# A transformer block kernel on Trainium2: low rotated keys padded with zeros to 128 rows, norms' projections in pairs, gathered rows used three steps behind their issue, spilled tiles from unit 9 on

## The chip, the cores and the metric

The kernel runs on one core of one Trainium2 chip. The metric is the device time of one execution in microseconds. Before the change it is 2821.38 us, the median of three runs (2819.73 to 2827.19).

## What is computed

The program takes a sequence of 512 tokens of width 1024 through three blocks. All arithmetic is in fp32, and the kernel keeps it by splitting each operand of a product into a high and a low part and adding three products.

1. A block with chunked gated linear attention, then a SwiGLU feed-forward.
2. A block with latent attention (MLA), then a SwiGLU feed-forward. The scores of a head are cut here to what the change touches:

```python
proj = h @ w_in
cq, ckv, k_rope = jnp.split(proj, [384, 640], axis=-1)
q_rope = apply_rope(q_rope, cos, sin)
k_rope = apply_rope(k_rope[:, :, None, :], cos, sin)[:, :, 0, :]
s = (einsum('bqhd,bkhd->bhqk', qn_b, k_nope) + einsum('bqhd,bkd->bhqk', qr_b, k_rope)) * scale
p = softmax(where(mask, s, -inf)); o = p @ v
```

The head has 128 unrotated and 64 rotated columns; the rotated key is shared by all 8 heads.

3. A block with a pooling and a convolution branch, and then a mixture of 16384 experts of one neuron each. Each token scores two sets of 128 keys per head (8 heads), takes the best 16 sums, and computes

```python
u = jnp.take(expert_u, experts, axis=0)
act = jax.nn.gelu(einsum('chkd,cd->chk', u, hc))
v = jnp.take(expert_v, experts, axis=0)
out = einsum('chk,chkd->cd', gate * act, v)
```

Adaptive layer norms (gain, shift and gate from a conditioning vector) stand ahead of every mixer and feed-forward; a final norm ends it.

## The kernel before

The activations lie with the width on the partitions and the tokens on the free axis, as 8 tiles `x[k]` of 128x512. `split` (L234) makes of an fp32 tile a high part by a cast on ACT and a low part by a subtraction on DVE (or on the engine `eng`). `mm3` (L274 to L276) multiplies in three matmuls: high by high, high weight by low input, low weight by high input. Weights stream in units of 1 MB: SP issues the load of `raw` (L267, and L1115 for the experts), and `parts` (L238) splits it in two halves, `whi` on ACT and `wlo` on DVE, both L240. There are two `raw` buffers, four `whi` and four `wlo`.

**Order of the work.** Each engine has a queue of its own, and a scheduler decides in which order the instructions stand in it; `high_priority` moves an instruction forward in it, `issue_after` holds one back. An engine works off its queue in order, so that an instruction which waits holds up all behind it.

**Norms.** `rsqrt` (L347) finds the inverse root of each token's mean square in three rounds of small DVE instructions (L355 to L357), `ry` and `rt` being 128x2. `bcast` (L365) spreads it over the partitions by PE transposes (L369). Then `modulated` makes `tmp`, `hh` and `hl` for the 8 input tiles (L424 to L426). `ahead` (L281) is the projection that follows a norm: four output tiles of it are computed while the norm of the second half of the tokens is still under way. It takes one bank after the other, with all 8 input tiles for each. Its weights' low parts are made by POOL (`eng=G_`). `ahead` is used at five sites; at the last, `w_query_2`, the table `POOL_LO` names POOL as well.

**Latent attention.** `norm_mla` rotates the shared key (L843 to L846) and splits it into `krh` and `krl`, 128x512 each, with the 64 rows twice, one copy for even and one for odd heads. `queries` (L865) makes for each head a tile `qs` which holds the high part in 64 rows and the low part in the other 64. `weigh` (L889) sums the scores of each block of 128 queries in five matmuls (L900 to L904); the third of them (L902) takes only the 64 rows `rr` of `qs` and `krl`. Softmax follows on DVE and ACT (L905 to L912), then the product with the values in `attend` (L915 to L931).

**Experts.** For the first 368 tokens the experts are computed densely. `up` (L1118) multiplies a unit of `ust` (256 experts) with the tokens, applies Gelu and keeps two tiles `a`. There is room for 16 of these (`NA`), so 8 units are computed ahead, and 12 later ones, in `SPILL`, are computed early, written to memory and brought back by `back` (L1132). The main loop (L1433) goes through 16 groups of 8 tiles: it loads the gates of the group into `gt` by SP (L1441), multiplies them into the tiles (L1443), splits these into `wh_` and `wl_` (L1444), and for each half of the output multiplies with two units of `vex` (`unit`, L1112) into four banks, which DVE then adds to `x` (L1462). After each half, `ups` computes or brings back two units for a later group.

**Gathered tokens.** The other 144 tokens take their experts' rows one at a time in `gathered` (L1352): POOL gathers `rows` by an indirect DMA (L1378), DVE multiplies with the token (L1382) in the first 144 steps, or adds into `y` (L1392) in the second 144. There are five `rows` buffers. `pace` (L1416) issues the steps evenly between the units, after a start of `FIRST = 3`.

## Time and profile before

| | |
|---|---|
| median of 3 runs | 2821.38 us (2819.73 to 2827.19) |
| profiled execution | 2822.08 us |
| its span in the trace | 2820.3 us |
| TensorE's mean granted clock | 0.986 |
| PE busy | 2706.4 us, 96% of the span, 14889 matmuls |
| DVE busy | 2107.8 us, 75% |
| ACT busy | 1072.3 us, 38% |
| POOL busy | 759.5 us, 27% |
| DMA | 560.62 MB, 199 GB/s in the mean |

The profile is of one execution. Times are microseconds from the start of its span; a line such as L902 is a line of the kernel before. PE is the matmul queue of TensorE, PEld its weight loads. Matmuls are pipelined, so their durations overlap, and the distance from start to start tells how fast they pass. The granted clock is a share of the full clock: TensorE has two levels, 1.2 and 2.4 GHz, so 0.83 over a window means that the lower one held for a third of it. An idle time stands in brackets ahead of the instruction that ended it, with what released it. The latent attention's heads lie at 750 to 880 us; the experts' selection and first group at 1900 to 2000 us; the main loop of experts from there to 2790 us.

### The profile page before, as it was taken

To read this page: it belongs to the slowest core of one execution; us is meant where nothing else is said; L and a number is where in the kernel's file an instruction comes from. 1 tells how busy PE (TensorE), PEld (TensorE's weight loads), DVE (VectorE), ACT (ScalarE), POOL (GpSimd) and SP (SyncE) were. 2 spreads that over 40 slices of the span, in tenths; PEclk is the share of its full clock that TensorE was granted. 3 is DMA by queue.
4 is the path that set the end of the run, shared out by engine and by line. 5 is a ranking of instruction groups with operands and counts; after the bars stand their busy time and mean duration, and the time that the engine had idled before them with its cause. 6 is when DMAs were issued, how large, how long until landed. Compare 5 with 4: busy or idle time off the path is not lost. (4 is left out here: it accounts for less than half of the span.)

```text
span 2820.3 us, 38954 instructions
## 1 busy us (share of the span) xinstructions
PE 2706.4 (96%) x14889; PEld 2435.0 (86%) x14889; DVE 2107.8 (75%) x4011; ACT 1072.3 (38%) x1530; POOL 759.5 (27%) x652
## 2 busy tenths in 40 slices
PE   6799999999999999999999999998899999999998
PEld 4677888888778888888888889998899999999998
DVE  8874755556776654548956897788998898888996
ACT  4443322223443322234443246653333333333332
POOL 4631100001011000001521410004555444445550
PEclk9999999999999999999999999999999999999999
DMA  6441355553212555522223236666999999988993
GB/s 262 148 137 60 135 193 180 189 191 109 75 45 75 179 181 177 181 88 91 90 90 105 77 125 211 208 201 254 345 347 352 351 335 329 349 335 319 350 350 130
DMA packets 184363, 560.62 MB, mean 199 GB/s; under 512 B 13248, under 2 KB 66912, under 8 KB 157680
## 3 DMA queue, kind: packets, MB, share of 16 engines
q1 hardware_dynamic: 128528, 356.74, 35.9%
q0 software_dynamic: 55296, 201.35, 19.7%
q8 instruction: 117, 1.92, 0.3%
q14 instruction: 70, 0.57, 0.1%
q10 hardware_dynamic: 352, 0.03, 0.0%
HBM read 527.32 MB, written 30.75 MB: 198 GB/s over the span
## 5 line engine op out<-in xcount | busy, mean ns | idle before, releaser
L240 ACT CAST whi<-raw 128x1024 fp32r<-128x1024 f32 x510 | 535.8, 1052 | 1260.8 <-PE mm L275 782.0
L275 PE MATMUL mm<-hl,whi 128*128 128x512 f32 (+2 forms) x2544 | 898.5, 354 | 9.7 <-DVE hl L426 8.9
L274 PE MATMUL mm<-hh,whi 128*128 128x512 f32 (+2 forms) x2544 | 898.2, 354 | 4.1 <-ACT hh L425 3.5
L276 PE MATMUL mm<-hh,wlo 128*128 128x512 f32 (+2 forms) x2544 | 897.1, 354 | 0.1
L240 DVE TENSOR_TENSOR wlo<-raw,whi 128x1024 fp32r<-128x1024 f32 x472 | 580.7, 1231 | 288.4 <-ACT whi L240 277.8
L275 PEld LDWEIGHTS mm<-hl,whi 128*128 128x128 f32 x2544 | 481.1, 189 | 58.4 <-DVE hl L426 10.7
L274 PEld LDWEIGHTS mm<-hh,whi 128*128 128x128 f32 x2544 | 480.7, 189 | 51.4 <-ACT hh L425 4.3
L276 PEld LDWEIGHTS mm<-hh,wlo 128*128 128x128 f32 x2544 | 481.1, 189 | 46.9 <-issue 0.8
L1378 POOL DMA_INDIRECT rows<-vex,eidx x144 | 219.3, 1523 | 210.2 <-DVE y L1392 192.5
L1378 POOL DMA_INDIRECT rows<-uex,eidx x144 | 209.2, 1453 | 214.6 <-DVE rows L1382 164.5
L319 POOL DMA_DIRECT2D araw<-ada x96 | 51.1, 533 | 555.4 <-DVE araw L312 538.1
L1392 DVE SCALAR_TENSOR_TENSOR y<-rows,act,y 128x1024 f32<-128x1024 f32 x142 | 181.3, 1277 | 7.4 <-DMA rows<-vex,eidx 6.9
L1382 DVE SCALAR_TENSOR_TENSOR rows<-rows,hn 128x1024 f32<-128x1024 f32 x144 | 170.0, 1219 | 15.4 <-DMA rows<-uex,eidx 15.4
L240 POOL TENSOR_TENSOR wlo<-raw,whi 128x1024 fp32r<-128x1024 f32 x38 | 91.2, 2405 | 279.2 <-ACT whi L240 234.4
L312 DVE SCALAR_TENSOR_TENSOR araw<-araw,sc 128x1024 f32<-128x1024 f32 x128 | 157.1, 1251 | 5.6 <-DMA araw<-ada 5.5
L275 PE MATMUL mm<-fl,whi 128*128 128x512 f32 (+1 forms) x396 | 145.1, 366 | 0.0
L276 PE MATMUL mm<-fh,wlo 128*128 128x512 f32 (+1 forms) x396 | 144.7, 365 | 0.0
L274 PE MATMUL mm<-fh,whi 128*128 128x512 f32 (+1 forms) x396 | 144.7, 365 | 0.0
L740 DVE TENSOR_TENSOR s<-s,mm 128x512 f32<-128x512 f32 x42 | 28.9, 688 | 133.6 <-PE mm L276 133.0
L448 DVE SCALAR_TENSOR_TENSOR x<-mm,mod,x 128x512 f32<-128x512 f32 (+1 forms) x66 | 43.9, 667 | 85.8 <-PE mm L276 85.7
L1311 ACT ACTIVATE stage<-acc 128x512 f32<-128x512 f32 x92 | 91.4, 1104 | 37.3 <-PE acc L1308 26.7
L1308 PE MATMUL acc<-oa,ob 128*128 128x128 f16 x736 | 101.6, 296 | 0.2
(1382 smaller groups left out, 4709.6 us busy)
## 6 DMA issues: line engine op xcount, KB each, us to landing
raw<-wst SPq DMA_DIRECT2D x127, 1024.0 KB, 5.0
raw<-ust SPq DMA_DIRECT2D x64, 1024.0 KB, 6.3
raw<-vex SPq DMA_DIRECT2D x64, 1024.0 KB, 7.4
araw<-ada POOLq DMA_DIRECT2D x96, 512.0 KB, 4.6
gd<-stage SPq DMA_DIRECT2D x23, 1024.0 KB, 4.6
gt<-gd SPq DMA_DIRECT2D x16, 1472.0 KB, 9.2
araw<-ada SPq DMA_DIRECT2D x32, 512.0 KB, 4.3
aw<-ada SPq DMA_DIRECT2D x16, 512.0 KB, 8.5
```

The source lines that it names most:

```text
L240: state["split"] = (A_.copy(hi, src), (eng or V).tensor_sub(lo, src, hi.bitcast(F32)))
L274: T_.matmul(out_, wh, ah, start=first, stop=False)
L275: T_.matmul(out_, wh, al, start=False, stop=False)
L276: state["mm"] = T_.matmul(out_, wl, ah, start=False, stop=last)
L312: op(out=w, in0=w, scalar=1.0, in1=sc, op0=ALU.mult, op1=ALU.mult, accum_out=out_)
L319: (G_ if l else SP).dma_start(raw, w[n * P:(n + 1) * P, :])
L448: return V.scalar_tensor_tensor(x[n][:, cs], p[:, cs], gate[:, n:n + 1], x[n][:, cs], op0=ALU.mult, op1=ALU.add)
L1308: T_.matmul(p[:, t * P:(t + 1) * P], ob[:, q, :, t], oa[i][:, q, :, t], start=i == 0, stop=i == 1)
L1311: A_.mul(st[:, :, t1:t1 + 4].rearrange("p j t -> p t j"), p.rearrange("p (t j) -> p t j", t=4), 1.0 / GSC)
L1378: G_.indirect_dma_start(out=r, out_offset=None, in_=uex if up_ else vex, in_offset=bass.IndirectOffsetOnAxis(ap=eidx[:, n:n + 1] if n < P ...
L1382: V.scalar_tensor_tensor(r, r, 1.0, hn if n < P else hx, op0=ALU.mult, op1=ALU.mult, accum_out=act[:, n:n + 1])
L1392: V.scalar_tensor_tensor(z, r, act[:, n:n + 1], z, op0=ALU.mult, op1=ALU.add)
```

## The change

Five things change; line numbers of the kernel after are two or three higher at first, 8 at `queries`, 16 and more in `gathered`.

1. **Low rotated keys.** `krl` becomes two tiles, in one buffer `kz` that has the tag `araw`. The one for even heads has zeros in rows 64 to 127, the one for odd heads in rows 0 to 63. L902 then multiplies all 128 rows. The subtraction is done in two pieces of 64 rows, and POOL writes the zeros.
2. **Projections of the norms.** `ahead` no longer names POOL for the low parts, so DVE makes them at four of the five sites (`POOL_LO` still holds at `w_query_2`). The four banks are computed in two pairs, with the input tile in the outer loop.
3. **Gathered rows.** Each step issues the gather of its row and uses the row that was issued `LAG = 3` steps before; `FIRST` is 4.
4. **Gates.** `gt` is loaded by ACT's queue, for the group after the one that was just multiplied. The products and splits have the priority `GPRI = 300`.
5. **Units.** `SPILL` is spread over units 16 to 63 in place of 8 to 63. The values of the experts come from `vst`, an array laid out on the host so that each partition's 8 KB of a unit are contiguous; before, four runs of 2 KB were read from `vex`.

```diff
+LAG = 3
+GPRI = 300
-FIRST = 3
+FIRST = 4
-SPILL = [NA // 2 + (2 * i + 1) * (P // 2 - NA // 2) // (2 * NSP) for i in range(NSP)]
+SPILL = [NA + (2 * i + 1) * (P // 2 - NA) // (2 * NSP) for i in range(NSP)]
...
-        ws = [[blk(name, eng=G_) for _ in ah] for _ in range(4)]
+        ws = [[blk(name) for _ in ah] for _ in range(4)]
...
-            for p, w in zip(pre, ws):
-                for k, (wh, wl) in enumerate(w):
-                    mm3(p[:, cs], wh, wl, ah[k][:, cs], al[k][:, cs], k == 0, k == len(ah) - 1)
+            for two in range(0, 4, 2):
+                for k in range(len(ah)):
+                    for p, w in zip(pre[two:two + 2], ws[two:two + 2]):
+                        mm3(p[:, cs], *w[k], ah[k][:, cs], al[k][:, cs], k == 0, k == len(ah) - 1)
...
-        krh, krl = [mp.tile([P, S], F32R, name=f"kr{i}") for i in range(2)]
-        split(krh, krl, kr)
+        krh = mp.tile([P, S], F32R, name="krh")
+        A_.copy(krh, kr)
+        kz = mn.tile([P, D], F32R, tag="araw", bufs=ARAW, name="kz")
+        krl = kz[:, :S], kz[:, S:]
+        for i, t in enumerate(krl):
+            on, off = slice(i * 64, i * 64 + 64), slice(64 - i * 64, 128 - i * 64)
+            G_.memset(t[off].bitcast(F32), 0.0)
+            V.tensor_sub(t[on], kr[on], krh[on].bitcast(F32))
...
-                T_.matmul(sc[:, :n], qx[rr, qs], krl[rr, :n], start=False, stop=False)
+                T_.matmul(sc[:, :n], qx[:, qs], krl[h % 2][:, :n], start=False, stop=False)
...
-                for i in range(2 * (P + EX)):
-                    n = i % (P + EX)
-                    up_ = i < P + EX
-                    r = ep.tile([P, D], F32, tag="rows", bufs=NROW, name="rows")
-                    G_.indirect_dma_start(out=r, out_offset=None, in_=uex if up_ else vex,
...
+                rows = []
+                for i in range(2 * (P + EX) + LAG):
+                    if i < 2 * (P + EX):
+                        n = i % (P + EX)
+                        r = ep.tile([P, D], F32, tag="rows", bufs=NROW, name="rows")
+                        G_.indirect_dma_start(out=r, out_offset=None, in_=uex if i < P + EX else vex,
...
+                        rows.append(r)
+                    if i < LAG:
+                        yield
+                        continue
+                    r = rows.pop(0)
+                    n = (i - LAG) % (P + EX)
+                    up_ = i - LAG < P + EX
...
-            per = (2.0 * (P + EX) - FIRST) / (todo - LAST)
+            per = (2.0 * (P + EX) + LAG - FIRST) / (todo - LAST)
...
+            def gate_load(g):
+                gt = er.tile([P, 3072], F32, tag="gt", bufs=1, name="gt")[:, :TD * JG] \
+                    .rearrange("p (s j t) -> p s j t", j=JG, t=TS)
+                A_.dma_start(gt, gd[g])
+                return gt
+            gt = gate_load(0)
...
-                        SP.dma_start(gt, gd[j // JG])
-                    V.tensor_mul(a, a, gt[:, :, j % JG, :])
-                    split(wh, wl, acts[j])
+                    with tc.high_priority(GPRI):
+                        V.tensor_mul(a, a, gt[:, :, j % JG, :])
+                        split(wh, wl, acts[j])
...
+                if g + 1 < P // GJ:
+                    gt = gate_load(g + 1)
...
-                        v = unit(vex[r0:r0 + 4 * P, half * 512:(half + 1) * 512]
-                                      .rearrange("(j p) d -> p j d", p=P), rearr=True)
+                        v = unit(vst[g * GJ // 4 + j4, half])
...
+        "vst": a["expert_v_2"][0].reshape(P // 4, 4, P, 2, 512).transpose(0, 3, 2, 1, 4).reshape(P // 4, 2, P, 2048),
```

The scheduler's order moves with it at three places.

On DVE, at the first norm that `ahead` follows (`rt`, `ry` the small tiles of the inverse root, `sa` the sum of squares, `tmp` and `hl` the modulated input, `wlo` a weight's low part), there stood before:

```order
L355 TENSOR_TENSOR rt<-ry 128x2
L356 TENSOR_TENSOR rt<-rt,rv 128x2
L357 SCALAR_TENSOR_TENSOR ry<-rt,ry 128x2
L395 TENSOR_TENSOR sa<-sa,sq 128x256
L424 SCALAR_TENSOR_TENSOR tmp<-x_84,sca,acc 128x256
L424 SCALAR_TENSOR_TENSOR tmp<-x_85,sca,acc 128x256
L424 SCALAR_TENSOR_TENSOR tmp<-x_86,sca,acc 128x256
L426 SCALAR_TENSOR_TENSOR hl_100<-tmp,mod_108,hh_92 128x256
```

and now:

```order
L358 TENSOR_TENSOR rt<-ry 128x2
L359 TENSOR_TENSOR rt<-rt,rv 128x2
L242 TENSOR_TENSOR wlo<-raw,whi 128x1024
L360 SCALAR_TENSOR_TENSOR ry<-rt,ry 128x2
L398 TENSOR_TENSOR sa<-sa,sq 128x256
L427 SCALAR_TENSOR_TENSOR tmp<-x_84,sca,acc 128x256
L427 SCALAR_TENSOR_TENSOR tmp<-x_85,sca,acc 128x256
L427 SCALAR_TENSOR_TENSOR tmp<-x_86,sca,acc 128x256
L427 SCALAR_TENSOR_TENSOR tmp<-x_87,sca,acc 128x256
L242 TENSOR_TENSOR wlo<-raw,whi 128x1024
L429 SCALAR_TENSOR_TENSOR hl_100<-tmp,mod_108,hh_92 128x256
```

Two subtractions of weights have come into DVE's row, one ahead of the last `ry`, one ahead of the first `hl`; before, POOL had them.

On DVE, at the start of the experts' main loop (`a` the activated tiles, which L1443 multiplies with the gates, `wl__` their low parts, and between them the last steps of the selection), there stood before:

```order
L240 TENSOR_TENSOR wlo<-raw,whi 128x1024
L1188 TENSOR_TENSOR g<-top 128x128
L1201 TENSOR_SCALAR du<-po 128x128 x2
L240 TENSOR_TENSOR wl__16343<-a,wh__16342 128x368
L1443 TENSOR_TENSOR a<-a,gt 128x368 x3
L1191 TENSOR_REDUCE sx<-g 128x8
L1443 TENSOR_TENSOR a<-a,gt 128x368
```

and now:

```order
L242 TENSOR_TENSOR wlo<-raw,whi 128x1024
L1196 TENSOR_TENSOR g<-top 128x128
L1209 TENSOR_SCALAR du<-po 128x128 x2
L1464 TENSOR_TENSOR a<-a,gt 128x368 x3
L242 TENSOR_TENSOR wl__16336<-a,wh__16335 128x368
L1199 TENSOR_REDUCE sx<-g 128x8
L1209 TENSOR_SCALAR du<-po 128x128
```

`wl__16336` is the low part of the group's first tile, and all eight products now stand ahead of it; before, `wl__16343` was the third tile's, and the first two had been split between the products.

On PE, around the first group's two halves (`acc<-wh__`, `acc<-wl__` the group's products, `mm<-hh_`, `mm<-hl_` an `up` unit for a later group). Before, 24 matmuls of `up` stood between the halves, and 48 between the second half and group 1, whose first tile is `wh__16870`:

```order
L276 MATMUL acc<-wh__16367,wlo 128x368
L274 MATMUL mm<-hh_92,whi 128x368
...
L276 MATMUL mm<-hh_99,wlo 128x368
L274 MATMUL acc<-wh__16330,whi 128x368
L275 MATMUL acc<-wl__16331,whi 128x368
...
L276 MATMUL mm<-hh_99,wlo 128x368
L274 MATMUL acc<-wh__16870,whi 128x368 x2
```

Now 79 stand between the halves, and 96 ahead of group 1, whose first tile is `wh__16944`:

```order
L278 MATMUL acc<-wh__16370,wlo 128x368
L278 MATMUL mm<-hh_97,wlo 128x368
...
L278 MATMUL mm<-hh_99,wlo 128x368
L276 MATMUL acc<-wh__16335,whi 128x368
L277 MATMUL acc<-wl__16336,whi 128x368
...
L278 MATMUL mm<-hh_99,wlo 128x368
L276 MATMUL acc<-wh__16944,whi 128x368
```

More of the units that are computed for later groups have come ahead of the second half and of group 1.

## Rows read from the trace of the kernel before

**Rows 1.** Page, part 1: engine, busy us (share of span), instructions.

```profile
PE 2706.4 (96%) x14889; PEld 2435.0 (86%) x14889; DVE 2107.8 (75%) x4011; ACT 1072.3 (38%) x1530; POOL 759.5 (27%) x652
```

**Rows 2.** Windows: stretch, its us, busy us (xcount) by engine, PEclk, DMA share, GB/s.

```profile
1900.00:1950.00 50.00, 44.74 (x263) 43.29 (x261) 43.19 (x134) 22.14 (x36) 12.44 (x15) 0.97 0.52 188
1950.00:2000.00 50.00, 36.81 (x191) 35.88 (x192) 43.02 (x71) 11.88 (x17) 26.40 (x20) 0.83 0.94 348
2000.00:2050.00 50.00, 50.00 (x302) 50.00 (x301) 45.37 (x74) 18.10 (x26) 27.21 (x19) 1.00 0.96 360
2700.00:2750.00 50.00, 50.00 (x302) 50.00 (x301) 46.38 (x53) 19.52 (x27) 26.89 (x17) 1.00 0.92 341
```

**Rows 3.** Timeline, PE, one block of scores: start us, us, engine, line, operation.

```profile
782.78 0.39 PE L900 MATMUL mm<-kn,qn 128*128 128x512 f32 x1
783.01 0.40 PE L901 MATMUL mm<-kr,qs 128*128 128x512 f32 x1
783.33 0.49 PE L902 MATMUL mm<-kr,qs 64*128 64x512 f32 x1
783.76 0.50 PE L903 MATMUL mm<-kn,qn 128*128 128x512 f32 x1
...
784.32 1.03 PE L923 MATMUL acc<-ct,pr 128*128 128x128 f32 x8
```

**Rows 4.** Timeline, PE, a projection of the same stage.

```profile
761.64 0.39 PE L275 MATMUL mm<-cl,whi 128*128 128x512 f32 x1
761.87 0.39 PE L276 MATMUL mm<-ch,wlo 128*128 128x512 f32 x1
```

**Rows 5.** Windows: the heads of attention.

```profile
760.00:880.00 120.00, 117.19 (x622) 93.85 (x622) 84.48 (x226) 46.37 (x100) 9.17 (x6) 1.00 0.11 37
```

**Rows 6.** Timeline, POOL, first norm.

```profile
310.12 2.34 POOL L240 TENSOR_TENSOR wlo<-raw,whi 128x1024 fp32r<-128x1024 f32 x1 [7.07 <-DVE rt L356]
```

**Rows 7.** Timeline, DVE, first norm.

```profile
309.57 0.15 DVE L357 SCALAR_TENSOR_TENSOR ry<-rt,ry 128x2 f32<-128x2 f32 x1
...
310.15 2.33 DVE L357 SCALAR_TENSOR_TENSOR ry<-rt,ry 128x2 f32<-128x2 f32 x1
```

**Rows 8.** Timeline, PE, first norm; in brackets the idle time before, and its releaser.

```profile
312.63 0.40 PE L369 MATMUL acc<-ct,ry 128*128 128x128 f32 x2 [2.23 <-DVE ry L357]
```

**Rows 9.** Page, part 5: the same subtraction on DVE, all of the span.

```profile
L240 DVE TENSOR_TENSOR wlo<-raw,whi 128x1024 fp32r<-128x1024 f32 x472 | 580.7, 1231 | 288.4 <-ACT whi L240 277.8
```

**Rows 10.** Windows: the four norm sites.

```profile
303.00:331.00 28.00, 23.84 (x193) 22.98 (x191) 22.68 (x63) 9.72 (x20) 4.77 (x3) 1.00 0.24 76
674.00:690.00 16.00, 11.15 (x76) 10.21 (x76) 15.04 (x28) 7.13 (x13) 7.29 (x3) 0.91 0.40 141
903.00:920.00 17.00, 13.67 (x107) 12.72 (x106) 14.54 (x37) 5.58 (x13) 4.78 (x2) 1.00 0.18 63
1267.00:1283.00 16.00, 11.02 (x79) 10.18 (x78) 15.53 (x44) 7.30 (x13) 7.49 (x7) 0.94 0.38 130
```

**Rows 11.** Timeline, DVE, the experts' start.

```profile
1908.29 0.52 DVE L1443 TENSOR_TENSOR a<-a,gt 128x368 f32<-128x368 f32 x1
...
1908.80 0.28 DVE L1163 FIND_INDEX8 ii<-vv,acc 128x8 uint32<-128x128 f32 x1
...
1943.48 1.23 DVE L1382 SCALAR_TENSOR_TENSOR rows<-rows,hn 128x1024 f32<-128x1024 f32 x1 [6.17 <-DMA rows<-uex,eidx]
...
1988.83 1.44 DVE L1443 TENSOR_TENSOR a<-a,gt 128x368 f32<-128x368 f32 x3
```

**Rows 12.** Timeline, PE, the experts' start.

```profile
1911.55 0.33 PE L274 MATMUL acc<-wh__16330,whi 128*128 128x368 f32 x1
...
1952.13 0.68 PE L274 MATMUL acc<-wh__16330,whi 128*128 128x368 f32 x1 [7.30 <-DVE x L1462]
...
1989.95 0.67 PE L274 MATMUL acc<-wh__16870,whi 128*128 128x368 f32 x1 [10.53 <-ACT wh__16870 L240]
```

**Rows 13.** Waits of SP's queue: us in total, times, longest us.

```profile
SPq L1441 <- DVE a L1443: 56.4, 15, 8.2
```

More of the change, by code (lines that the diff above doesn't have):

```diff
@@ L193, in block_kernel @@
 @with_exitstack
-def block_kernel(ctx, tc, x_in, cs_in, wst, vec, cst, gmask, smask, pos, ada1, ada2, wgate, keys, ust, uex, vex, out):
+def block_kernel(ctx, tc, x_in, cs_in, wst, vec, cst, gmask, smask, pos, ada1, ada2, wgate, keys, ust, uex, vst, vex, out):
     nc = tc.nc
@@ L358, in rsqrt, with colsums @@
         return y
-    def colsums(p, col, s, width):
+    def colsums(p, col, s, width, start=True, stop=True):
         for c in range(s.shape[-1] // P):
-            T_.matmul(p[:, col + c:col + c + 1], s[:, c * P:(c + 1) * P], inv[width], start=True, stop=True)
+            T_.matmul(p[:, col + c:col + c + 1], s[:, c * P:(c + 1) * P], inv[width], start=start, stop=stop)
     def bcast(y):
@@ L893, in weigh @@
             qx = qrot.pop(h)
-            rr = slice(h % 2 * 64, h % 2 * 64 + 64)
             prs = []
@@ L1110, in block_kernel, with unit @@
         spilled = dr.tile([2 * NSP, P, TD], F32, name="spilled")
-        def unit(src, rearr=None, eng=None):
+        def unit(src, eng=None):
             with tc.high_priority(AHEAD):
                 raw = wp.tile([P, 2048], F32, tag="raw", bufs=RAW, name="raw")
-                SP.dma_start(raw.rearrange("p (j d) -> p j d", j=4) if rearr else raw, src)
+                SP.dma_start(raw, src)
                 return parts(raw, eng)
@@ L1431, in ups @@
                         nu += 1
+            def gate_load(g):
[3 more added lines that the diff above has]
+                return gt
+            assert GJ == JG
+            gt = gate_load(0)
             for g in range(P // GJ):
```

8 lines of the change are left out of this document (2 added, 6 removed).

## The prediction

> **What bounds the kernel now.** I read the page's busy shares first. TensorE is busy for 2706.4 us, 96% of the span [rows 1], so a change can only gain where PE stands still, runs at the lower of its two clock levels, or issues its matmuls further apart than their columns need. Next come the windows, and the reader should look at the count beside PE's busy time. From 2000 us on, PE issues 302 matmuls in 50 us at a granted clock of 1.00, one every 0.166 us, and the window from 2700 us reads the same [rows 2]: nothing is to be had there, whatever becomes of DVE, the queues or the DMA. In the two windows before, where the experts begin, only 263 and 191 matmuls were issued, and the second has a granted clock of 0.83 [rows 2]. That is 39 + 111 = 150 matmuls short, 150 x 0.166 = 24.8 us. The other two places that the change touches are the attention and the norms.
>
> **Padding the low rotated keys.** In PE's timeline of one block of scores the reader should look at the starts, not at the durations, which overlap. Of five 512-column matmuls the first four start at 782.78, 783.01, 783.33 and 783.76, and the work after the fifth starts at 784.32 [rows 3]: 1.54 us for five. In a projection a little earlier, where every matmul has 128 rows, starts are 0.23 us apart [rows 4], so five would take 1.15 us. It is the 64-row matmul (783.33) and the one after it that start late: 0.39 us is lost around each. There are 8 heads x 4 blocks = 32 of them, and if the narrower blocks lose as much, 12.5 us is the most that the padding can return. It returns it only where PE sets the pace. From 760 to 880 us PE is busy 117.2 of 120 us and DVE 84.5 [rows 5], so I expect most of it, and take **10 us**; the bounds are 0 (the softmax's chain takes over) and 12.5. The Trainium skill ("TensorE: Matmul & The Clock Gate", "Why this matters for your kernels") says that a matmul over 32 rows takes as long as one over 128, so that few rows cost or save nothing by themselves; by it this term would be 0 and the sum 2807. The starts in [rows 3] speak against reading it so when full-height matmuls stand on both sides. The cost side: one 128-row subtraction becomes two of 64 rows and two memsets go to POOL, all beside PE's work on the latent norm; at DVE's 0.7 us for 512 columns this is at most 0.7 us once, and it goes into the rounding.
>
> **The norms' projections.** In the first norm POOL subtracts a weight chunk from 310.12 for 2.34 us [rows 6]. DVE's `ry`, a two-column instruction that takes 0.15 us, was started at 310.15 and took 2.33 [rows 7]: it was held for as long as POOL ran. PE stood idle 2.23 us for that `ry` [rows 8]. The change does the same subtraction on DVE, which takes 1.23 us [rows 9] instead of holding it for 2.2, so each collision on the norm's chain shortens by about 1.0 us. At the four sites (the fifth keeps POOL) I count ten collisions, and PE is idle 4.2, 4.9, 3.3 and 5.0 us there, from the busy times in [rows 10]: 17.4 us together. Ten collisions less 1.0 us each would give 10 us if PE followed DVE fully. The six subtractions which today collide with nothing now cost DVE time as well, so I take half, **5 us**. The new order of the matmuls (pairs of banks, with the input tile in the outer loop) asks for each `hl` tile half as often, which points the same way. Bounds: 0, since DVE's order shows a subtraction right before the last `ry` and another before the first `hl`, and 10.
>
> **The experts' start.** Two waits make up most of the 24.8 us. PE is idle 7.30 us up to 1952.13, where half 1 of the first group wants banks which DVE has not yet emptied, and 10.53 us up to 1989.95, where group 1 wants its gated activations [rows 12]. Both come from DVE standing in its queue: at 1943.48 it had waited 6.17 us for the first gathered row, and the gate products of group 1 start only at 1988.83, behind a row of gathers [rows 11]. The change acts on both. Rows are used three steps after their issue, so the first use no longer stands ahead of the emptying of the banks; gate products and splits get a priority, and they read a `gt` that was fetched a group ahead. And PE gets filler: 79 matmuls between the halves instead of 24, and 96 before group 1 instead of 48, which is 9.1 and 8.0 us more of cover at 0.166 us each.
>
> It also makes new waits. All eight products of group 0 now stand ahead of the first split. From 1908.73 there remain seven at 0.44 us and two subtractions at 1.14 us, both from start to start, and a dozen selection steps of 0.1 to 0.3 us [rows 11], 3.1 + 2.3 + 2.6 = 8.0 us, so the first low half is done at about 1917.2; PE comes for it four matmuls after 1911.55, at 1912.2: 5.0 us of idleness where there is none today. Going on like this through DVE's new order gives waits of about 1.2, 0.4 and 3 us more, 9.6 us in all, and I add 3 us for the lower clock, which in this stretch followed each of the long idle times. So 24.8 - 12.6 = 12.2 us; as such a replay forgets waits more often than it invents them, I take **10 us**. Bounds: 3 (the new waits are twice as long) and 18 (only the first exists).
>
> **Costed at nothing.** That a partition's 8 KB of a `v` unit come as one run instead of four of 2 KB concerns the DMA, which costs PE nothing after 2000 us [rows 2]; the cover is the second `raw` buffer, and with slower DMA casts would start late. The units spilled are as many as before, only later ones. The gate load goes from SP's queue to ACT's: SP waited there 15 times, 56.4 us in all, longest 8.2 [rows 13], and what is behind it now are ACT's casts, by which PE gets its weights. One cast feeds 24 matmuls, 4.0 us, and four are buffered, so waits of 8 us are covered if the buffers are full. The tail after 2790 us stays.
>
> **Sum.** 10 + 5 + 10 = 25 us off the profiled execution's 2822.1: 2797 us. The profiled execution stands 0.7 us over the median of the runs, 2821.4, which is within the rounding, so I forecast **2797 us**. A measurement of this kernel can tell about 0.3% from no change, 8.5 us: faster means under 2813, slower over 2830.
>
> **Rivals.**
> - *The padding gives nothing.* DVE's chain of maximum, exponential and scaling would set the head's time and PE would idle where it now issues slowly. For it: PE already waits for DVE now and then in the heads. Against it: DVE is busy 70% there [rows 5]. 2797 + 10 = 2807 us. It is also where the Trainium skill's rule would lead.
> - *The idle time at the experts' start only moves forward.* All new waits double and the clock falls with them: 2797 + 10 = 2807 us, a little more if the collision with selection grows. For it: DVE's order does put eight products ahead of the first split.
> - *Both of these*: 2817 us, no change that can be told.
> - *DVE's subtractions cost the norms what POOL's did*: 2802 us.
> - *ACT stands behind the gate load* (slower). The load of a group must wait for the last product of the group before it, and the casts behind it on ACT stop with it. If the 56.4 us of [rows 13] were paid by PE in full, 15 times 3.8 us, the time would be 2797 + 56 = 2853 us. It decides from 1.7 us paid per load (25 us in 15 loads), and passes "slower" from 2.3. Against it: the four buffered casts, and that SP comes to its wait as soon as it has nothing ahead of it, which ACT need not.
> - *The new waits don't come*, as the products find their place in DVE's gaps: 2797 - 8 = 2789 us.
>
> **How the numbers follow.** Forecast 0.46, padding without effect 0.12, idle time moved 0.16, norms without gain 0.05, no new waits 0.06: faster, 0.85 together. Both of the first two rivals, 0.08: same. ACT behind the gate load, 0.07: slower. The range runs from 2784 (12.5 + 10 + 15, near the upper ends at once) to 2818 (the two rivals together); it leaves out the ACT rival and the tails of the others.
>
> **What would show it.** In the profile after: the five starts of a 512-column block within 1.15 us; no two-column DVE instruction of 2.3 us at the four sites, and about 12 us of PE idleness there instead of 17; a new wait of some 5 us near 1912 us of today's count, and none of 7 and 10 us behind it, with fewer than 80 matmuls missing in the 100 us. Wrong would be: a head as long as before, DVE instructions that still take over 2 us beside POOL, windows after the experts' start with fewer than 302 matmuls per 50 us, or PE waiting for ACT's casts near each gate load.

## The result and the profile after

The kernel after takes 2803.79 us, the median of five runs (2800.60 to 2807.24); the kernel before took 2821.38 us in five runs beside it. The ratio is 0.9943, with a 95% interval of 0.9929 to 0.9956: 16 us faster by the ratio, 17.6 by the medians. Three single executions of the kernels in this document took 5.3, 9.3 and 11.1 ms; they stand outside all ratios and ranges. The profiled execution took 2807.13 us, its span is 2805.4 us against 2820.3, so 14.9 us are to be found in the traces. It is the slowest but one of the five.

The page's line of the engines, the answer to [rows 1], has PE busy for the same 96%:

```profile
PE 2699.4 (96%) x14889; PEld 2438.1 (87%) x14889; DVE 2095.0 (75%) x4028; ACT 1059.9 (38%) x1530; POOL 741.4 (26%) x638
```

To place the 14.9 us I took the start of the same piece of work in both timelines of PE: the first score matmul, the last value matmul, the first product of each group of experts, the last matmul. In the experts I also counted the 368-column matmuls between two such starts in PE's order and took 0.1667 us for each; what a stretch lasts beyond that is its loss.

| stretch | before | after | difference |
|---|---|---|---|
| up to the first score matmul | 751.0 us | 750.6 us | -0.3 |
| the heads, to the last value matmul | 111.3 us | 98.5 us | -12.7 |
| from there to the first product of the experts | 1049.3 us | 1047.7 us | -1.5 |
| groups 0 and 1 of the experts, loss | 24.7 us | 10.8 us | -13.9 |
| groups 2 to 14, loss | 0.0 us | 12.6 us | +12.6 |
| last group and tail, loss | 11.0 us | 12.0 us | +1.0 |

The sum is 14.8 us. The heads and the start of the experts each gave more than was forecast; the norms gave little; and nearly all that the start of the experts gained is lost again in the main loop, a stretch in which the kernel before lost nothing.

**The heads.** PE's timeline of a block of scores in the kernel after, the answer to [rows 3] (L908 to L912 are now the five matmuls):

```profile
776.16 0.39 PE L908 MATMUL mm<-kn,qn 128*128 128x512 f32 x1
776.39 0.40 PE L909 MATMUL mm<-krh,qs 128*128 128x512 f32 x1
776.62 0.40 PE L910 MATMUL mm<-kz,qs 128*128 128x512 f32 x1
776.86 0.39 PE L911 MATMUL mm<-kn,qn 128*128 128x512 f32 x1
...
777.32 1.03 PE L931 MATMUL acc<-ct,pr 128*128 128x128 f32 x8
...
802.33 0.40 PE L908 MATMUL mm<-kn,qn 128*128 128x512 f32 x1
```

Five matmuls take 1.16 us where they took 1.54. The same block two heads later starts at 802.33, 26.17 us on. In the kernel before it was 28.60 us, from 782.78 [rows 3] to:

```profile
811.38 0.40 PE L900 MATMUL mm<-kn,qn 128*128 128x512 f32 x1
```

That is 2.43 us for two heads, 9.7 us for eight. The other 3 us go with the clock, as the windows of the heads show, first of the kernel after, then of the one before:

```profile
747.00:852.00 105.00, 100.74 (x592) 85.69 (x591) 82.20 (x234) 46.09 (x105) 12.80 (x9) 1.00 0.14 46
```

```profile
750.00:863.00 113.00, 109.21 (x572) 86.00 (x573) 81.30 (x231) 44.14 (x102) 11.48 (x8) 0.97 0.11 38
```

The granted clock was 0.97 over the heads before and is 1.00 now. In the trace before, TensorE goes to its lower level for 6.8 us at 752.1, within the first head; in the trace after it does not.

**The norms.** The windows of the four sites, the answer to [rows 10], each near the same piece of work:

```profile
303.00:331.00 28.00, 25.12 (x193) 24.20 (x192) 20.45 (x65) 9.66 (x20) 0.00 (x0) 0.94 0.22 76
674.00:690.00 16.00, 15.97 (x131) 15.62 (x130) 14.17 (x43) 7.30 (x13) 0.00 (x0) 1.00 0.41 148
891.00:908.00 17.00, 14.51 (x105) 13.75 (x104) 13.27 (x41) 6.15 (x13) 0.00 (x0) 0.90 0.19 63
1254.00:1271.00 17.00, 16.19 (x128) 15.32 (x128) 15.44 (x60) 8.19 (x15) 0.32 (x4) 1.00 0.38 129
```

POOL is out of them, and PE is idle for 2.9, 0.0, 2.5 and 0.8 us, 6.2 in place of 17.4. These windows flatter the change: those of the second and the fourth site end just ahead of a wait that belongs to the site.

```profile
691.31 0.40 PE L372 MATMUL acc<-ct,ry 128*128 128x128 f32 x2 [1.10 <-DVE ry L360]
...
1273.12 0.40 PE L372 MATMUL acc<-ct,ry 128*128 128x128 f32 x2 [1.30 <-DVE ry L360]
```

Counted from one spread of `ry` over the partitions to the next, PE is idle for 2.8, 1.1, 2.5 and 2.1 us, 8.5 in place of 17.5, and the four stretches are 7.7 us shorter. The fifth site keeps POOL's subtractions, and there the collision of [rows 6, 7] appears in the kernel after, where the kernel before had none; PE's line stands below DVE's:

```profile
1517.74 2.35 DVE L360 SCALAR_TENSOR_TENSOR ry<-rt,ry 128x2 f32<-128x2 f32 x1
1520.24 0.40 PE L372 MATMUL acc<-ct,ry 128*128 128x128 f32 x2 [2.23 <-DVE ry L360]
```

The first two sites, 3.1 us shorter together, lie ahead of the first score matmul; yet the stretch up to it is only 0.3 us shorter. PE's timeline shows where the gain went, a new wait at the norm of the latent queries:

```profile
728.82 1.09 PE L372 MATMUL acc<-ct,ry 128*128 128x128 f32 x4 [3.92 <-DVE ry L360]
```

and DVE's timeline shows why:

```profile
724.40 0.15 DVE L360 SCALAR_TENSOR_TENSOR ry<-rt,ry 128x4 f32<-128x4 f32 x1
...
725.77 1.23 DVE L242 TENSOR_TENSOR wlo<-raw,whi 128x1024 fp32r<-128x1024 f32 x1
...
727.52 0.69 DVE L849 TENSOR_TENSOR kr<-kr,tmp 128x512 f32<-128x512 f32 x1
...
728.51 0.16 DVE L360 SCALAR_TENSOR_TENSOR ry<-rt,ry 128x4 f32<-128x4 f32 x1
```

The last round of `ry` starts at 728.51, 4.1 us after the one before it at 724.40, as a weight's subtraction, rotations of the key (`kr`) and low parts of the latents stand between them in DVE's queue. PE's timeline has the second site 3.3 us shorter (from 677.9 to 694.8 us before, from 677.7 to 691.3 after, between two spreads of `ry`); nearly all of that is lost from there to the first score matmul, where this wait stands, with the clock at its lower level for 3.4 us from 728.8.

**The start of the experts.** The windows, the answer to [rows 2]:

```profile
1900.00:1950.00 50.00, 46.04 (x258) 45.37 (x259) 43.42 (x92) 18.49 (x31) 21.58 (x15) 0.94 0.76 281
1950.00:2000.00 50.00, 50.00 (x299) 49.82 (x298) 47.44 (x74) 12.96 (x18) 31.86 (x21) 1.00 0.95 354
2000.00:2050.00 50.00, 49.65 (x296) 49.34 (x295) 47.72 (x73) 20.16 (x30) 25.11 (x19) 1.00 0.94 359
2700.00:2750.00 50.00, 48.03 (x284) 47.40 (x283) 48.01 (x58) 19.51 (x28) 25.30 (x18) 1.00 0.90 337
```

The work lies 15 us earlier in these stretches than in [rows 2], but that PE issues 299 matmuls in the second where it issued 191 is plain. PE's two waits of 7.30 and 10.53 us [rows 12] are gone; these two stand at the start of group 0:

```profile
1896.91 0.94 PE L276 MATMUL acc<-wh__16335,whi 128*128 128x368 f32 x4 [0.87 <-ACT wh__16335 L242]
1901.56 0.68 PE L277 MATMUL acc<-wl__16336,whi 128*128 128x368 f32 x1 [3.71 <-DVE wl__16336 L242]
```

Waits of 0.34 and 2.05 us follow in the same group, and its granted clock is at the lower level for 6.8 us from 1899.5. The second wait shown is the one for the first low half, which DVE begins behind the eight products at 1900.98:

```profile
1900.98 0.53 DVE L242 TENSOR_TENSOR wl__16336<-a,wh__16335 128x368 fp32r<-128x368 f32 x1
```

**The main loop.** One window of the kernel before, then three of the kernel after:

```profile
2100.00:2300.00 200.00, 200.00 (x1202) 200.00 (x1201) 177.26 (x272) 70.97 (x96) 99.54 (x67) 1.00 0.94 348
```

```profile
2100.00:2300.00 200.00, 198.42 (x1182) 198.12 (x1181) 171.56 (x265) 69.02 (x97) 102.87 (x68) 1.00 0.92 342
2300.00:2500.00 200.00, 199.77 (x1190) 199.35 (x1189) 178.45 (x220) 70.39 (x102) 110.19 (x68) 1.00 0.92 336
2500.00:2700.00 200.00, 199.04 (x1184) 198.22 (x1183) 175.37 (x197) 66.75 (x96) 108.69 (x68) 1.00 0.93 341
```

In 200 us the kernel before issued 1202 matmuls; the kernel after 1182, 1190 and 1184. Two things add up. Every group from 2 on loses 0.4 us although PE shows no idle time: its starts on the group's products are 170.7 ns apart where the weights change from one triple of a product to the next, and 167.7 and 168.2 within a triple, where all of them were 166.6 before (the mean of a group). That is 6.6 ns for each of 64 triples, 0.42 us. And five of the thirteen groups lose 0.3 to 2.7 us more, in real waits. From 2030 to 2790 us, where PE had none in the kernel before, these are PE's waits:

```profile
PE acc L276 <- DVE x L1483: 3.4, 5, 1.7
PE mm L278 <- DVE wlo L242: 1.6, 1, 1.6
```

They are for DVE, which empties the banks late or makes a weight's low part late; none is for a cast of ACT. The other engines' waits of the main loop in the kernel after:

```profile
ACT whi L242 <- DMA raw<-vst: 161.1, 38, 8.3
ACT whi L242 <- DMA raw<-ust: 148.5, 23, 10.8
...
DVE y L1408 <- DMA rows<-vex,eidx: 45.4, 13, 5.9
...
DVE rows L1398 <- DMA rows<-uex,eidx: 38.7, 14, 5.6
ACT whi L242 <- DVE a L1464: 36.4, 6, 8.0
```

Before, ACT's casts waited 125 us for units of `vex` and 34 us for units of `ust`, and DVE 3 + 7 us for gathered rows.

One of the losses can be followed. ACT, then DVE, then PE:

```profile
2100.71 0.33 ACTq L1452 DMA_DIRECT2D gt<-gd  x1
2101.16 2.00 ACT L242 CAST whi<-raw 128x1024 fp32r<-128x1024 f32 x2 [6.96 <-PE acc L278]
2112.72 2.00 ACT L242 CAST whi<-raw 128x1024 fp32r<-128x1024 f32 x2 [9.56 <-DMA raw<-ust]
```

```profile
2100.14 0.54 DVE L1464 TENSOR_TENSOR a<-a,gt 128x368 f32<-128x368 f32 x1
...
2113.03 1.23 DVE L1398 SCALAR_TENSOR_TENSOR rows<-rows,hn 128x1024 f32<-128x1024 f32 x1 [5.50 <-DMA rows<-uex,eidx]
...
2116.58 1.23 DVE L1398 SCALAR_TENSOR_TENSOR rows<-rows,hn 128x1024 f32<-128x1024 f32 x1 [2.32 <-DMA rows<-uex,eidx]
```

```profile
2119.01 0.43 PE L278 MATMUL mm<-hh,wlo 128*128 128x368 f32 x1 [1.58 <-DVE wlo L242]
```

The gate load could be issued only when DVE's last product of the group was done, at 2100.68, and the two casts behind it started at 2101.16, after ACT had been idle for 6.96 us (the profile names a product of PE as what ended this, but the gate load stands ahead of the casts in ACT's queue). The gates' 1.5 MB then travelled beside a unit that SP had issued at about 2100.2: the casts of that unit started at 2112.72, over 12 us after its issue, where the page has a median landing of 7.1 us for such a unit. DVE meanwhile waited 5.50 and 2.32 us for gathered rows, with the subtraction that PE needed behind them. PE stood 1.58 us. So here PE waited for DVE behind gathered rows; that the gates' transfer made the rows late is a reading of the times, which no run tried by itself.

### The profile page after: what moved, and what is told of

Read it like the earlier page. It is cut to its first block, busy times and chain, and to the rows that moved or that the text cites. A ratio compares the mean times of both kernels' runs of the same rounds, so it can differ in the third digit from the quotient of the medians.

```text
span 2805.4 us, 38971 instructions
## 1 busy us (share of the span) xinstructions
PE 2699.4 (96%) x14889; PEld 2438.1 (87%) x14889; DVE 2095.0 (75%) x4028; ACT 1059.9 (38%) x1530; POOL 741.4 (26%) x638
## 4 chain that ended last, share of the span: by engine, by line
PE 60%; DVE 14%; issue 12%; POOL 8%; DMA 5%; ACT 1%; POOLq 0%; SPq 0%; DVEq 0%; ACTq 0%
PE mm L277 15%; PE mm L276 15%; PE mm L278 15%; POOL rows L1387 7%; PE acc L1316 3%; DMA rows<-vex,eidx 3%; DVE wlo L242 3%; PE acc L278 2%; PE acc L277 2%; PE acc L276 2%; PE acc L646 1%; DMA rows<-uex,eidx 1%; PE acc L365 1%; DVE aw L481 1%; PE acc L935 1%
## 5 line engine op out<-in xcount | busy, mean ns | idle before, releaser
L242 DVE TENSOR_TENSOR wlo<-raw,whi 128x1024 fp32r<-128x1024 f32 x488 | 598.9, 1231 | 234.6 <-ACT whi L242 223.6
L1387 POOL DMA_INDIRECT rows<-vex,eidx x144 | 233.0, 1618 | 193.8 <-DVE y L1408 176.4
L1316 PEld LDWEIGHTS <-ob 128*128 128x128 f16 x736 | 76.8, 118 | 13.5 <-DVE oa L1307 0.6
```

Source lines behind the costliest of these rows:

```text
L242: state["split"] = (A_.copy(hi, src), (eng or V).tensor_sub(lo, src, hi.bitcast(F32)))
L1316: T_.matmul(p[:, t * P:(t + 1) * P], ob[:, q, :, t], oa[i][:, q, :, t], start=i == 0, stop=i == 1)
L1387: G_.indirect_dma_start(out=r, out_offset=None, in_=uex if i < P + EX else vex, in_offset=bass.IndirectOffsetOnAxis(ap=eidx[:, n:n + 1] if ...
```

## The experiments

Each kernel was compared with the kernel before, run beside it. Ratios have 95% intervals.

**The padding alone** (the kernel before with this edit):

```diff
-        krh, krl = [mp.tile([P, S], F32R, name=f"kr{i}") for i in range(2)]
-        split(krh, krl, kr)
+        krh = mp.tile([P, S], F32R, name="krh")
+        A_.copy(krh, kr)
+        kz = mn.tile([P, D], F32R, tag="araw", bufs=ARAW, name="kz")
...
-                T_.matmul(sc[:, :n], qx[rr, qs], krl[rr, :n], start=False, stop=False)
+                T_.matmul(sc[:, :n], qx[:, qs], krl[h % 2][:, :n], start=False, stop=False)
```

> The kernel before with the padded low rotated keys alone. Theory A (the 64-row matmul costs PE about 0.4 us per block of scores, and nothing downstream takes it back): the heads go from 111.3 us (first score matmul to last value matmul, before) to 98.5 us as in the kernel after, and the whole is 12 to 13 us faster than before. Rival (part of the gain in the heads depends on the other edits, or is lost later): under 8 us faster.

Measured: ratio 0.9956 (0.9942 to 0.9970), 2807.3 us against 2822.1. The heads took 98.5 us. The gain is that of the heads, 12.4 us by the ratio (14.8 by the medians): theory A holds. In its profile groups 10 and 11 lost 0.6 and 1.6 us, the second after DVE had waited 6.8 us for gates, which SP loads here without a lead; so the loop can lose a little with the gates on SP too.

**The norms alone**:

```diff
-        ws = [[blk(name, eng=G_) for _ in ah] for _ in range(4)]
+        ws = [[blk(name) for _ in ah] for _ in range(4)]
...
+            for two in range(0, 4, 2):
+                for k in range(len(ah)):
...
```

> The kernel before with the change of the norms' projections alone (low parts by DVE, pairs of banks). Theory A (what PE gains at a norm is lost again a little later, as the scheduler's new order lets the chain of the next norm wait on DVE): within 2 us of before. Rival (the norms give what was forecast, and other edits took it back): 5 us faster or more, with PE idle times above 0.4 us at the four sites down from 17 us to 8 or less.

Measured: ratio 0.9990 (0.9981 to 0.9999), 2.8 us, between the two expectations. The four sites' idle times above 0.4 us fell to 7.3 us, as the rival said, but the wait at the latent queries' norm is there as well, so it belongs to this edit:

```profile
729.54 1.09 PE L370 MATMUL acc<-ct,ry 128*128 128x128 f32 x4 [3.92 <-DVE ry L358]
```

The heads took 111.3 us in this run, as before.

**The edits to the experts alone** (the kernel after with the old norms and unpadded keys):

> The kernel after with the old norms' projections and the unpadded keys: of the change only the edits to the experts stand (lag, priority, gate load on ACT, later spilled units, contiguous values). Theory A (the start of the experts gains about 14 us, the main loop and the selection give it all back in small losses per group): within 3 us of before, PE's wait at the start of group 0 about 9.6 us less its ideal, and every group from 2 on longer than 56.0 us by 0.4 or more. Rival (the start's gain stays and the small losses come from the other two edits): 8 us faster or more, groups of 56.0 us.

Measured: ratio 1.0018 (1.0008 to 1.0029), 5 us slower. Group 0 lost 9.6 us, as in the kernel after, so the start's gain is there; group 1 lost 3.5, the groups from 2 on 0.4 each, four of them 0.5 to 2.3 more and group 14 5.5 more. These edits by themselves made the kernel slower, and the three parts add up to the whole within their uncertainty: -12.4 - 2.8 + 5.1 = -10 us, each uncertain by 2.5 to 4, against -16 (by 4).

**The width of the gates' tile** (the kernel after with this edit):

```diff
-                gt = er.tile([P, 3072], F32, tag="gt", bufs=1, name="gt")[:, :TD * JG] \
+                gt = er.tile([P, 3064], F32, tag="gt", bufs=1, name="gt")[:, :TD * JG] \
```

> The kernel after with the tile for the gates 3064 columns wide instead of 3072, as before, nothing else. In the kernel after each matmul on the group's products that changes weights starts 4 ns late (170.7 instead of 166.7 ns after the one before), 0.4 us per group. Theory B (the width shifts the addresses of the tiles that lie behind it, and the matmuls read those at a worse place): starts return to 166.7 ns, about 6 us faster than the kernel after. Rival (the slip comes from the traffic, as values now arrive in 8 KB runs or gates are read by another queue): starts as in the kernel after, and no change over 2 us.

Measured: ratio 0.9961 (0.9946 to 0.9977), no faster than the kernel after, groups of 56.4 us at best. A miss; but this edit had moved the gates' tile, by 32 bytes, and not `wh_` and `wl_`. As every engine does the same work in the same order, the run is nearly a second profile of the kernel after: group 0 lost 9.6 us in both, and groups 1 to 14 lost 27.5 us here and 13.8 there. The irregular losses differ from execution to execution.

**A 32-byte tile behind the low parts** (the kernel after with this edit):

```diff
+                if g == 0:
+                    V.memset(er.tile([P, 8], F32, name="pad"), 0.0)
```

> The kernel after with a 32-byte tile allocated behind the low parts of the group's products, nothing else: the tiles wh_ and wl_ then begin at multiples of 64 bytes in a partition, as they do in the kernel before, and not 32 bytes past one, as in the kernel after and in the run with the 3064 columns (which moved the gates' tile but not these two). Theory B (refined: the place of the moving operand modulo 64 bytes makes the 4 ns): groups without another wait last 56.0 us, starts 166.7 ns apart, 5 to 7 us faster than the kernel after. Rival (traffic): 56.4 us as before, no gain.

Measured: ratio 0.9970 (0.9957 to 0.9982), 2812.6 us; the groups without another wait still last 56.4 us. The place modulo 64 bytes does not make the loss, but it decides where it falls: the starts at a change of weights are 167.0 ns apart here, and those within a triple 170.0 and 169.3. The run is also slower than the kernel after. The tile was not "nothing else": it needs a `memset` on DVE, and with it the order of the first group's work changed on ACT, DVE and PE. In this order the first group lost 18.1 us, most of the excess in one wait and in some 10 us more at the lower clock:

```profile
1953.54 0.43 PE L278 MATMUL acc<-wh__16355,wlo 128*128 128x368 f32 x1 [4.16 <-DVE wlo L242]
```

Single groups of the loop lost up to 4.2 us, and the runs lay between 2801.6 and 2821.4 us. The next three runs carry this tile, so they are to be compared with this one and not with the kernel after.

**The gates by SP's queue, with this tile**:

```diff
-                A_.dma_start(gt, gd[g])
+                SP.dma_start(gt, gd[g])
```

> The same with the gates loaded by SP's queue instead of ACT's, still a group ahead. Theory C (in the main loop ACT stands behind the gate load, which waits for DVE's last product, and PE then waits for weights): ACT's waits for the products of DVE vanish from the list (36.4 us, 6 times, in the kernel after), PE's losses in the groups from 2 on fall by half or more, 2 to 5 us faster than with the aligned tiles alone. Rival (the losses come from DVE, which waits for gathered rows, or from the loads' own time): the same within 2 us; or slower, as the load of weights now queues behind the wait on SP.

Measured: ratio 0.9943 (0.9930 to 0.9957), 2804.1 us, 8.4 us less than with the tile alone and more than theory C asked for. Groups 1 to 13 lose 0.4 us, none more, and group 14 0.6. ACT's waits for DVE's products are gone.

**No lag** (the 32-byte tile, `LAG = 0`, `FIRST = 3`):

> The aligned kernel with a lag of 0 and three steps at first: each gathered row is used in the step that issues it, as before. Theory D (the lag moved the uses from a place that the scheduler chose late to a fixed one, and DVE now waits for rows in the main loop: 45 + 39 us against 7 + 3 before): DVE's waits for rows fall to 20 us or less after 2000 us, the groups' losses fall, and at the experts' start PE's first long wait of the kernel before comes back by 3 us or more. Rival (the lag is what makes the start short and costs nothing later): DVE's waits do not fall, the start loses 5 us or more, the whole is slower than the aligned kernel by that.

Measured: ratio 0.9946 (0.9931 to 0.9961). DVE still waited 35 + 29 us for rows, so theory D falls: the lag did not make these waits. Nor did it make the start: groups 0 and 1 lost 12.2 + 2.2 us, less than with the tile and a lag of 3 (18.1 + 0.4), and the long waits did not come back. In its profile groups 2 to 13 lost 0.4 us each and no more, with ACT still loading the gates; group 14 lost 2.5. The whole is some 7 us faster than with the lag (2803.2 us against 2812.6), where the rival expected it slower: in this pair the lag costs time.

**The old array of values** (the 32-byte tile, units from `vex` in runs of 2 KB):

> The aligned kernel with the experts' values read from the old array in four runs of 2 KB per partition. Theory E (runs of 8 KB move as fast as runs of 2 KB here, the median landing of a unit was 7.8 us before and 7.5 after in the main loop): within 2 us of the aligned kernel. Rival 1 (the long runs help): slower by 3 us or more, with landings of 8 us and over. Rival 2 (the long runs crowd the gathered rows out, which land 0.3 to 0.9 us later than before): faster by 2 us or more, gathered rows landing in 7.1 to 7.4 us again.

Measured: ratio 0.9966 (0.9954 to 0.9978), the same as with the long runs (0.9970), as theory E says; its trace holds no landings, so that part was not read. Every engine's order is that of the run with the tile alone. Groups 2 to 13 lost 0.4 us each here too, group 14 2.6, and the first group 20.7 us.

**The gates by SP's queue alone** (the kernel after with the edit from `A_` to `SP` shown above, no added tile):

> The kernel after with one edit: the gates are loaded by SP's queue instead of ACT's (no added tile). Theory C (ACT behind the gate load makes the main loop's irregular losses, which differ from execution to execution): no group from 2 on loses more than 0.6 us in the profile, ACT's waits for DVE's products are gone from the list, and the time is 3 to 6 us below the kernel after, with a smaller spread between its runs. Rival (the aligned tile, or chance, made the run with SP's queue clean): groups that lose 1 to 4 us as in the kernel after, no gain.

Measured: ratio 0.9942 (0.9928 to 0.9955), 2805.4 us, five runs from 2804.1 to 2805.9. Theory C holds for the loop: no group from 2 to 13 loses more than 0.4 us, ACT waits once for a product of DVE, 2.6 us, and the waits of the main loop are short:

```profile
DVE y L1408 <- DMA rows<-vex,eidx: 19.2, 12, 2.9
ACT whi L242 <- DMA raw<-vst: 19.0, 4, 8.0
DVE rows L1398 <- DMA rows<-uex,eidx: 13.2, 7, 2.6
...
ACT whi L242 <- DMA raw<-ust: 3.9, 1, 3.9
```

ACT's waits for units fell from 310 us to 23. The gain of 3 to 6 us did not come. Against the profile of the kernel after, groups 2 to 14 lose 7.0 us less, but the start takes 3.9 us back and the last group and tail 0.7; that profile is also 3.3 us above its kernel's median. At the start the first load on SP brought another order, and PE waits 5.60 us for the first product instead of 0.87:

```profile
1900.67 1.59 PE L276 MATMUL acc<-wh__16335,whi 128*128 128x368 f32 x4 [5.60 <-ACT wh__16335 L242]
```

**And the gates' tile behind the products** (so that `wh_` and `wl_` lie where they lie in the kernel before):

```diff
-                gt = er.tile([P, 3072], F32, tag="gt", bufs=1, name="gt")[:, :TD * JG] \
+                gt = er.tile([P, 3064], F32, tag="gt", bufs=1, name="gt")[:, :TD * JG] \
...
-            gt = gate_load(0)
+            gt = None
...
+                    if gt is None:
+                        gt = gate_load(0)
```

> The same, and the gates' tile is allocated behind the group's products, 3064 columns wide, so that wh_ and wl_ lie at the addresses that they have in the kernel before (192512 and 204800 in a partition). Theory F (the 4 ns per change of weights come from where these tiles lie, by whole kilobytes and not by the 32 bytes that the aligned run corrected): groups of 56.0 us, starts 166.7 ns apart, about 6 us faster than with SP's queue alone. Rival (they come from how the order of the work or the traffic has changed): 56.4 us, the same time within 2 us.

Measured: ratio 0.9920 (0.9907 to 0.9932), 2798.5 us, 6.9 us less than the run with SP's queue alone, on the same chip. Every group from 1 to 13 takes exactly what its matmuls need, and the starts are 166.7 ns apart in the mean. The windows, first of the run with SP's queue alone, then of this one:

```profile
2100.00:2300.00 200.00, 200.00 (x1194) 200.00 (x1193) 172.85 (x264) 71.95 (x97) 99.50 (x68) 1.00 0.93 347
```

```profile
2100.00:2300.00 200.00, 200.00 (x1202) 200.00 (x1201) 174.23 (x267) 72.84 (x99) 100.06 (x69) 1.00 0.93 349
```

Theory F holds: in both traces every engine does the same work in the same order, and only the addresses of `wh_`, `wl_` and the gates' tile, which PE does not read, differ. So 8 matmuls in 200 us, 1.3 us, come from where the moving operands lie. Before and here `wh_` begins at 192512 and `wl_` at 204800 bytes in a partition; in the kernel after both lie some 12 KB higher. Which of the two tiles makes the loss, and by what rule, stays open. This kernel has the lowest time of all that were run, and is faster than both the kernel before and the kernel after.

**No priority** (gates by SP's queue, `GPRI = 0`):

> The kernel after with gates by SP's queue and without the priority of the products and splits (0 instead of 300). Theory G (the priority is what makes the start of group 1 early and also what sets eight products ahead of the first split): the wait of some 5 us near the start of group 0 goes, PE's long waits before half 1 or group 1 come back, the first group loses 15 us or more against 10, and the whole is 5 us or more slower than with SP's queue alone. Rival (the filler alone hides the waits, and the priority only costs): the first group loses 8 us or less, faster by 2 us or more.

Measured: ratio 0.9938 (0.9926 to 0.9950). In its profile the first group lost 12.5 us against 10.5: neither expectation. The priority is worth 2 us there at most, and nothing in the whole. As the lag is not what shortened the start either, two edits are left: the filler that the later spilled units bring (the first one is unit 18, where it was 10; the title's unit 9 is a slip), and the gates loaded a group ahead. Neither was tried by itself, nor the priority and the lag left out together.

**The first gate load by ACT, the others by SP** (on top of the tile behind the products):

```diff
-                SP.dma_start(gt, gd[g])
+                (SP if g else A_).dma_start(gt, gd[g])
```

> As the run with the gates' tile behind the products, but the first of the 16 gate loads is issued by ACT's queue, as in the kernel after, the other 15 by SP's. In the profiles PE waits 5.6 us for the first group's first product when SP issues the first load, and 0.9 us when ACT does. Theory H (the queue of the first load, and the order that the scheduler builds around it, sets that wait): it falls back to 1 us, the first group still loses about 10 us, the later ones nothing, and the whole is 3 to 5 us faster than with all 16 on SP, about 2794 us. Rival (the wait belongs to the selection on DVE and only shows at another place): within 2 us of it, 2797 to 2800 us.

Measured: ratio 0.9927 (0.9911 to 0.9943), 2801.6 us, no gain. The wait at the start fell as theory H says, but the whole went as the rival has it, since group 1 then lost 9.4 us, 5.0 of it in one wait, with 6.8 us at the lower clock from 2015.5:

```profile
1896.94 0.95 PE L276 MATMUL acc<-wh__16333,whi 128*128 128x368 f32 x4 [0.88 <-ACT wh__16333 L242]
1901.59 0.68 PE L277 MATMUL acc<-wl__16334,whi 128*128 128x368 f32 x1 [3.70 <-DVE wl__16334 L242]
...
2017.25 0.67 PE L278 MATMUL acc<-wh__16964,wlo 128*128 128x368 f32 x1 [4.96 <-DVE wlo L242]
```

## Why the prediction was right, and where not

The time lies in the range, and the direction was right; the forecast was 2797 us and the result 2803.8. That it came out so near is in part luck: of the three terms the padding carried nearly all of the result. The edits to the experts, from which 10 us were forecast, cost 5 by themselves, and 3 us of the padding's gain came with a clock that nobody had forecast. Point by point:

- **The padding**, forecast 10 us with an upper bound of 12.5: 12.7 in the trace and 12.4 by the run with it alone. The mechanism was the one named: 0.38 us less for each block of 512 columns, 9.7 us for the heads. The rest is a stretch at the lower clock which all three profiled kernels with unpadded keys show near 752 us (the kernel before, the norms alone, the experts alone), and none with padded ones. The forecast had not counted it. The Trainium skill ("TensorE: Matmul & The Clock Gate", "Why this matters for your kernels") gives a single matmul over 32 rows the time of one over 128; read as a rule for a 64-row matmul between full ones it fails here: with one five took 1.54 us, without 1.16.
- **The norms**, forecast 5 us: 2.8 by the run with them alone (0.3 to 5.4, which still holds the 5). At the four sites the collisions with POOL went as said; PE's idle time there fell by 9 us and the sites became 7.7 us shorter, more than the 5 forecast. The reason for the halving was misread: of the six subtractions said to collide with nothing four (at 295, 301, 888 and 894 us) hold a sum of squares, which takes 0.68 us alone, for over 2.3 us. What the term left out is the way from a site to the end: the new order made the chain of the latent queries' norm wait for 3.92 us on DVE, and the selection's first search (1556 us) for 2.1; and the collision came up at the fifth site.
- **The start of the experts**, forecast 24.8 us lost before, 9.6 us of new waits and 3 us of clock after, 10 to 12 us gained. Group 0 lost 9.6 us, clock included, in the kernel after and in the run with these edits alone: waits of 3.71, 0.34 and 2.05 us, and 6.8 us at the lower clock, which cost some 3.4. That 9.6 is also the forecast's sum of the waits alone is chance. Group 1 lost another 1.2. The gain was 13.9 us. The replay of DVE's order by durations of the trace was right for the first low half (a wait of 3.7 us for it behind 0.9 for the high half, where 5.0 was forecast). But the loss at the start moves with small changes of the order: with the 32-byte tile and the lag it was 18 and 21 us in two profiles.
- **What was costed at nothing** is the step that failed: "nothing is to be had there" from 2000 us on. Nothing could be gained, but there was something to lose, 12.6 us in groups 2 to 14. Some 5 us of it are the few ns by which products start late since the gates' tile was allocated ahead of theirs, a cost that no row of before could show and that the sum did not think of. The other 7 are waits, which the rival "ACT stands behind the gate load" foresaw in part: with the gates on SP they are gone from groups 2 to 13 in five profiles. Its price was far off, 7 us in the profile of the kernel after and not 56, and so was its path: in these groups PE waited for DVE, which stood behind gathered rows or came late to the banks, and never for ACT's casts. Whether the casts in store covered the rest, as the prediction has it, no run shows.
- The chance of 0.07 for slower was about this rival. For the edits to the experts by themselves its sign came true (1.0018, 2828 us, not past the 2830 that the forecast calls slower), and the padding paid for it.

What is not settled is the cause of the irregular losses. With the new order and ACT loading the gates, four profiles of six have them in groups 2 to 13 and all six in group 14, 2.5 to 5.9 us; with SP loading them, none of five has (0.3 to 0.7 us in group 14). So ACT's gate load takes part in them, but not in every execution: they were absent up to group 13 with no lag and with the old array, and one profile of each kernel cannot tell whether these edits gave the loop room or whether that execution was a lucky one. Nor is it the only way to them, as the 2.1 us of the run with the padding alone show. Whether ACT's queue or the moment of the gate load matters more, and why the rows come late to DVE, was not separated.

## What to carry to other kernels

Look for short matmuls between full ones in the starts of PE's timeline; padding one operand with zeros costs two memsets and gave 12 us here. In a loop in which PE is full, ask of every edit what it can lose: a load moved to a queue that also computes puts its wait ahead of that engine's work, and a tile allocated in another order moves its neighbours. A gain at one wait counts only once the next wait on the same engine's queue has been looked at.

## What the runs showed of the hardware

- A matmul over 64 rows between matmuls over 128 rows costs 0.38 us more for the five at 512 columns (1.54 and 1.16 us). It shows in the starts: its own and the two behind it come 0.1 to 0.2 us late [rows 3].
- Where the moving operands lie in a partition changed the pace of fp32 matmuls with 368 columns: three of them took 500 ns from start to start at one place and 506 to 507 at a place 12 KB higher. 32 bytes less there left the sum as it was and moved the late starts from the change of weights (170.7 ns, then 167.0) to within the triple (167.7 and 168.2, then 170.0 and 169.3).
- A two-column DVE instruction that takes 0.15 us took 2.33 us when a POOL subtraction of 128x1024 had started 0.03 us before it [rows 6, 7]; without that POOL work the kernel after shows no such instruction at the four sites, and at the fifth, which keeps it, one of 2.35 us.
